# First conditioning round in two quarters and a half, and the filter network's middle layer moved

## The chip, the cores and the metric

The kernel runs on one core of one Trainium2 chip. The metric is device time of one execution in microseconds (us); lower is better. Engines in the text: PE multiplies matrices (PEld is its weight loading), DVE and ACT work element by element, POOL is a slower general engine, and SP issues the loads. Each engine takes its instructions in one fixed order, and an instruction whose input is late holds up everything behind it on that engine.

## The reference

One layer of a sequence model, over 512 latent tokens x and 256 context tokens of width 1024. The part that matters here is its beginning:

```python
mod = (silu_c @ w_ada[l] + b_ada[l])[:, None, :]
sh1, sc1, g1, sh2, sc2, g2 = jnp.split(mod, 6, axis=-1)
modc = silu_cc @ w_ada[l] + b_ada[l]
csh1, csc1, cg1, csh2, csc2, cg2 = jnp.split(modc, 6, axis=-1)
hc = rmsnorm(ctx_s, norm1_g[l]) * (1.0 + csc1) + csh1
khc, vhc, lgc = project_kvg(hc, lp, seq_conv)
st_f, st_b = context_states(khc, vhc, lgc)
h = rmsnorm(x, norm1_g[l]) * (1.0 + sc1) + sh1
kh, vh, lg = project_kvg(h, lp, lat_conv)
y = mixer(h, kh, vh, lg, st_f, st_b, lp, lat_conv, hyena_spectra(seq_len, lp))
```

`mod` is the conditioning: a vector from c times the wide matrix `w_ada`. Its first two sixths, the shift `sh1` and the scale `sc1`, are needed before h exists, and h feeds every projection. `hyena_spectra` runs a small filter network (three layers, each a product followed by a sine) over 512 positions and turns its output into spectra; it does not depend on x. Everything after the mixer (merge, output projection, gated feed-forward part, last norm) stays as it is.

## The kernel before, in words

**Layout.** x lies transposed in eight tiles `xt[k]` of 128 features by 512 tokens (buffers `uh`, `ul`). A product of fp32 precision is made of three products of split numbers: a number is split into a rounded high half and the rest, its low half, and `gemm` (L555) issues for each of the eight k high times high (L215), high weight times low input (L216) and low weight times high input (L217). So h needs a high half `hTh` (ACT, L1071) and a low half `hTl` (DVE, L1077, from an intermediate that DVE makes at L1076), and each weight tile needs a high half `wh` (ACT) and a low half `wl` (DVE).

**Conditioning.** Rows of `w_ada` for shift and scale are 4 MB. They come in two halves of 16 pieces of 256 KB: the first half serves the features of k = 0 to 3, the second those of k = 4 to 7. `ada_load` (L301) issues the loads of a half, into buffers that are free at that time (`hTh`, `hTl` and `K` for the first half; `hTh`, `hTl`, `dih`, `dil`, `gx1`, `cx2` for the second). `ada_first` (L315) multiplies them with the silu of c and of the context's c: 32 products 256 columns wide (64 matmul instructions in a trace), four side by side in PE's columns. ACT copies the result, PE transposes it twice (L328), DVE adds the bias into `modT` (L335) and makes the scale `amod` (L336).

**Start of x.** ACT squares the eight tiles, DVE adds the squares (L385), PE sums over the partitions with a matrix of ones (L388), DVE and POOL form the reciprocal root (L371, L373), PE spreads it over all partitions into the bank `xb` (L375), and DVE multiplies x by it (L1040 for k = 0 to 3, L1101 for k = 4 to 7).

**Query tiles.** The first four query weight tiles (0 to 3) are held in PSUM and made in two parts each: `part(i, 0)` takes k = 0 to 3, as soon as the first conditioning half is there, `part(i, 1)` takes k = 4 to 7. Each part is twelve matmuls. Between the first parts stand the first products of the filter spectrum (L445, L446) and the second half of conditioning; before its second use DVE normalises k = 4 to 7.

**Filter network.** `filter_network` (L392) is a generator: at each `next` it issues the sine of the layer before, the matmul of the next layer, and six dependent DVE operations (L407 to L412). The last layer is twice as wide as the first two. Its result, the stack, is what L445 and L446 multiply with the weights `w4`. The table of the transform (`fr`, split into `fh` and `fl`) is needed by the spectrum's later products only.

**What sets the order.** The program is written as one sequence. A planner then gives each engine its own fixed order: among the instructions of which it believes the inputs ready, the one that stands first in the program goes. `tc.issue_after(ins)` binds the instructions of its block that run on the engine of `ins` to come behind `ins` there, without a wait for its result. `behind(lag)` (L560) is the same for the last matmul of the list `tails`, to which `gemm` adds the last matmul of each call. Loads are issued by SP in program order.

## Time and profile before

| | |
|---|---|
| three runs | 1227.28, 1228.36, 1229.19 us (median 1228.36) |
| profiled execution | 1230.75 us |
| its span, first to last instruction | 1228.9 us |
| granted clock of PE, mean | 0.99 |
| PE busy | 1189.2 us, 97% |
| DVE busy | 834.1 us, 68% |
| ACT busy | 528.3 us, 43% |
| chain that ended last | PE 88%, DVE 5%, DMA 3% |

A row of the timeline reads: start in us from the beginning of the span, length in us, engine, line of the kernel, operation, tile written and tiles read, shapes, how many instructions of this kind follow each other, and, in brackets, how long the engine stood idle before and what ended that. Neighbouring instructions overlap by about a tenth of a microsecond. PEclk is the share of full speed that PE's clock was granted.

### The profile page before, as it was taken

To read this page: it belongs to the slowest core of one execution; us is meant where nothing else is said; L and a number is where in the kernel's file an instruction comes from. 1 tells how busy PE (TensorE), PEld (TensorE's weight loads), DVE (VectorE), ACT (ScalarE), POOL (GpSimd) and SP (SyncE) were. 2 spreads that over 40 slices of the span, in tenths; PEclk is the share of its full clock that TensorE was granted. 3 is DMA by queue.
4 is the path that set the end of the run, shared out by engine and by line. 5 is a ranking of instruction groups with operands and counts; after the bars stand their busy time and mean duration, and the time that the engine had idled before them with its cause. 6 is when DMAs were issued, how large, how long until landed. Compare 5 with 4: busy or idle time off the path is not lost.

```text
span 1228.9 us, 16765 instructions
## 1 busy us (share of the span) xinstructions
PE 1189.2 (97%) x6440; PEld 1014.0 (83%) x6440; DVE 834.1 (68%) x1336; ACT 528.3 (43%) x824; POOL 69.1 (6%) x131
## 2 busy tenths in 40 slices
PE   4999999999999999999999989999999999999997
PEld 2799988888888888888777878889888888888886
DVE  5967797978989899796767777667654344332332
ACT  3754466754445545354665633233423223222321
POOL 0011110100010000101001112000000000000000
PEclk9999999999999999999998999999999999999998
DMA  9644452463333443335645556773452332333312
GB/s 351 238 163 156 140 190 95 146 228 132 106 126 120 138 162 104 133 108 205 202 150 184 162 181 206 266 265 120 138 154 87 103 100 89 99 91 98 95 47 70
DMA packets 60689, 182.73 MB, mean 149 GB/s; under 512 B 8376, under 2 KB 12224, under 8 KB 58432
## 3 DMA queue, kind: packets, MB, share of 16 engines
q1 hardware_dynamic: 53264, 153.33, 38.5%
q0 software_dynamic: 7344, 28.32, 6.3%
q8 instruction: 51, 0.84, 0.3%
q14 instruction: 30, 0.25, 0.1%
HBM read 151.21 MB, written 30.41 MB: 148 GB/s over the span
## 4 chain that ended last, share of the span: by engine, by line
PE 88%; DVE 5%; DMA 3%; issue 2%; ACT 2%; POOL 0%; SPq 0%; DVEq 0%; POOLq 0%; ACTq 0%
PE bank L215 26%; PE bank L216 26%; PE bank L217 25%; PE bank L641 2%; PE bank L642 2%; PE bank L643 2%; DMA s<-hhd 1%; DMA wr<-in_wph 1%; PE bank L445 1%; PE bank L598 1%; PE bank L446 1%; DMA hmd<-s 1%; PE bank L319 1%; DVE wl L212 1%; DMA ul<-in_xT 0%
## 5 line engine op out<-in xcount | busy, mean ns | idle before, releaser
L215 PE MATMUL bank<-hTh,wh 128*128 128x512 f32 (+1 forms) x952 | 368.6, 389 | 7.5 <-DVE den L945 2.9
L216 PE MATMUL bank<-hTl,wh 128*128 128x512 f32 (+1 forms) x952 | 367.2, 387 | 2.0 <-DVE hTl L1077 2.0
L217 PE MATMUL bank<-hTh,wl 128*128 128x512 f32 (+1 forms) x952 | 367.0, 386 | 0.0
L211 ACT ACTIVATE wh<-wr 128x1024 fp32r<-128x1024 f32 (+1 forms) x167 | 172.1, 1032 | 407.9 <-PE bank L216 202.9
L212 DVE TENSOR_TENSOR wl<-wr,wh 128x1024 fp32r<-128x1024 f32 (+1 forms) x167 | 197.9, 1188 | 175.2 <-ACT wh L211 174.1
L215 PEld LDWEIGHTS bank<-hTh,wh 128*128 128x128 f32 x952 | 179.3, 189 | 43.6 <-issue 4.3
L216 PEld LDWEIGHTS bank<-hTl,wh 128*128 128x128 f32 x952 | 179.4, 189 | 36.7 <-DVE hTl L1077 2.5
L217 PEld LDWEIGHTS bank<-hTh,wl 128*128 128x128 f32 x952 | 179.4, 189 | 35.2
L216 PE MATMUL bank<-big,wh 128*128 128x512 f32 (+1 forms) x266 | 94.8, 356 | 0.0
L215 PE MATMUL bank<-big,wh 128*128 128x512 f32 (+1 forms) x266 | 94.7, 356 | 0.0
L217 PE MATMUL bank<-big,wl 128*128 128x512 f32 (+1 forms) x266 | 94.6, 356 | 0.0
L354 DVE SCALAR_TENSOR_TENSOR wr<-wr,crow 128x1024 f32<-128x1024 f32 x32 | 39.0, 1221 | 33.5 <-DMA wr<-in_wada 33.5
L216 PEld LDWEIGHTS bank<-big,wh 128*128 128x128 f32 x266 | 50.3, 189 | 7.1
L215 PEld LDWEIGHTS bank<-big,wh 128*128 128x128 f32 x266 | 50.3, 189 | 7.1
L217 PEld LDWEIGHTS bank<-big,wl 128*128 128x128 f32 x266 | 50.3, 189 | 7.1
L211 ACT ACTIVATE hb<-hb 128x512 fp32r<-128x512 f32 (+1 forms) x49 | 36.7, 768 | 28.0 <-DVE hb L450 17.7
L1525 DVE TENSOR_TENSOR s<-s,bank 128x512 f32<-128x512 f32 x22 | 15.1, 687 | 46.4 <-PE bank L217 46.4
L212 DVE TENSOR_TENSOR hb<-hb,hb 128x512 fp32r<-128x512 f32 (+1 forms) x49 | 40.3, 859 | 2.0 <-ACT hb L211 1.8
L643 PE MATMUL bank<-wh,hTl 128*128 128x256 f32 (+1 forms) x128 | 36.5, 285 | 0.0
L641 PE MATMUL bank<-wh,hTh 128*128 128x256 f32 (+1 forms) x128 | 36.5, 285 | 0.0
L642 PE MATMUL bank<-wl,hTh 128*128 128x256 f32 (+1 forms) x128 | 36.4, 284 | 0.0
L373 POOL TENSOR_TENSOR rr<-rv,negh 128x2 f32<-128x2 f32 (+1 forms) x6 | 5.5, 924 | 509.1 <-DVE rv L371 509.1
(376 smaller groups left out, 2194.0 us busy)
## 6 DMA issues: line engine op xcount, KB each, us to landing
wr<-in_win SPq DMA_DIRECT2D x64, 512.0 KB, 3.7
wr<-in_w SPq DMA_DIRECT2D x60, 512.0 KB, 3.6
wr<-in_wada SPq DMA_DIRECT2D x32, 512.0 KB, 4.4
Kd<-K POOLq DMA_DIRECT2D x8, 1024.0 KB, 4.7
K<-Kd SPq DMA_DIRECT2D x8, 1024.0 KB, 5.6
wr<-in_wv SPq DMA_DIRECT2D x8, 512.0 KB
gmd<-s POOLq DMA_DIRECT2D x16, 256.0 KB, 2.6
wr<-in_wph SPq DMA_DIRECT2D x8, 512.0 KB, 3.5
```

What stands on the lines that cost most here:

```text
L211: act.activation(hi, x, AF.Copy)
L212: dve.tensor_sub(lo, x, hi.bitcast(F32))
L215: pe.matmul(o, wh, xh, start=first, stop=False)
L216: pe.matmul(o, wh, xl, start=False, stop=False)
L217: return pe.matmul(o, wl, xh, start=False, stop=last)
L319: m = pe.matmul(ps[32 * g : 32 * g + 32, :256], silc[:, k, :], units[k, g], start=bool(k == 0), stop=bool(k == KT - 1))
L354: dve.scalar_tensor_tensor(w, w, 1.0, crow[:], op0=ALU.mult, op1=ALU.mult, accum_out=s)
L445: pe.matmul(ps[:], lhs, w4h, start=True, stop=False)
L641: pe.matmul(o, xh, wh, start=bool(k == 0), stop=False)
L642: pe.matmul(o, xh, wl, start=False, stop=False)
L643: m = pe.matmul(o, xl, wh, start=False, stop=bool(k == KT - 1))
L1525: dve.tensor_tensor(t[:], t[:], pb[:], op=ALU.mult)
```

## The change

The rows of `w_ada` for the first half are laid out as two quarters of eight pieces. Quarter 0 serves k = 0 and 1, quarter 1 serves k = 2 and 3; the second half (now parts 2 and 3 of the loads) stays whole. A quarter has 32 products of 128 columns, one transpose and one addition. Loads are issued in the order quarter 0, query tile 0, quarter 1, query tiles 1 to 3, spectrum vectors, second half, transform table, context.

In the program the middle layer of the network now stands ahead of quarter 0, and the last square, the sums and the broadcast are bound behind the transpose of quarter 0 on PE. x is normalised and h is made in pieces of two k. Tile 0's first part is cut in two (k = 0, 1 and k = 2, 3). The network's last layer is bound behind the first of these on PE. The second half's conditioning products stand behind tile 3's first part and the spectrum's first products in the program and are bound only behind tile 2's; the split of the transform table moves behind the high and low halves of k = 4 to 7.

```diff
-    w = a["w_ada"][0][:, :2048].reshape(4, 2, 128, 2, 2, 2, 256)
-    c["wada1"] = w.transpose(4, 0, 3, 2, 5, 1, 6).reshape(2, 4, 2, 128, 4, 256)
+    w = a["w_ada"][0][:, :2048].reshape(KT, 128, 2, 2, 2, 256)
+    q = w[:, :, :, 0].transpose(3, 0, 1, 2, 4).reshape(2, KT, 128, 512)
+    h = w[:, :, :, 1].reshape(KT, 128, 2, 512).transpose(2, 0, 1, 3)
+    c["wada1"] = np.concatenate([q, h], 0)
...
+    def ada_load(part):
+
+        for k in range(KT):
+            dma(aslots[part][k], I["wada1"][part, k])
+
+    def ada_first(part, p, tag):
+
+        n = 1 if part < 2 else 2
         ps = bank()
         for k in range(KT):
             for g in range(4):
...
+                u = aslots[part + (g // 2 if n == 2 else 0)][k]
+                c0 = 128 * n * (g % 2 if n == 2 else g)
+                pe.matmul(
+                    ps[32 * g : 32 * g + 32, : 128 * n], silc[:, k, :], u[:, c0 : c0 + 128 * n], start=bool(k == 0), stop=bool(k == KT - 1)
                 )
...
+        tails.append(mark.ins)
...
+    ada_load(0)
+    load_q(0)
+    ada_load(1)
+    for i in range(1, NQ):
+        load_q(i)
+    dma(w4r, I["hw4"][sp[0]].rearrange("p f n -> p (f n)"))
+    dec, skip = spectrum_vectors(PH, *sp[0])
+    ada_load(2)
+    ada_load(3)
+    dma(fr, I["dftf"])
...
+    for k in range(KT - 1):
         sq_sums(ax_, xt[k], k, 4, PH, "s2", sums)
     next(network)
-    ahead(AH[0])
+    am = ada_first(0, PH, "s2")
     xb = bank()
-    rms_bcast(sums[:, :4], 4, xb, PH, "s2")
-    next(network)
-    ahead(AH[1])
-    for k in range(4):
-        dve.tensor_tensor(xt[k], xt[k], xb[:], op=ALU.mult)
+    with behind():
+        sq_sums(ax_, xt[KT - 1], KT - 1, 4, PH, "s2", sums)
+        rms_bcast(sums[:, :4], 4, xb, PH, "s2")
...
-    high, low = modulated(0)
+    norm(0, 2)
+    list(early_split(0))
+    high, low = modulated(0, 2)
+    norm(2, 4)
+    ada_first(1, PH, "s2")
     qps = [bank(psG) for _ in range(NQ)]
     with tc.issue_after(high), tc.issue_after(low):
+        part(0, 0, 2)
+        high, low = modulated(2, 4)
+    with behind():
+        next(network)
+    with tc.issue_after(high), tc.issue_after(low):
         list(early_split(1))
+        list(early_split(2))
+        part(0, 2, 4)
+        part(1, 0, 4)
+        part(2, 0, 4)
         stack = next(network)
+        list(early_split(3))
...
+        norm(4, KT)
+        part(3, 0, 4)
     sp0 = spectrum(*sp.pop(0), (dec, skip, (w4s[:, 0], w4s[:, 1])))
-    for i in range(AQ):
-        part(i, 0)
-    next(sp0)
-    ada = ada_first(PH, 1, units[1], "s2")
-    tr, am, copy = ahead(8)
-    for i in range(AQ, NQ):
-        part(i, 0)
-    with tc.issue_after(high), tc.issue_after(low):
-        split(fh[:], fl[:], fr)
-    high, low = modulated(1)
+    with behind():
+        next(sp0)
+    with tc.issue_after(tails[-2]):
+        ada_first(2, PH, "s2")
+    high, low = modulated(4, KT)
...
     with tc.issue_after(high), tc.issue_after(low):
-        part(0, 1)
+        split(fh[:], fl[:], fr)
+        part(0, 4, KT)
...
```

116 lines of the change are left out of this document (38 added, 78 removed).

## The prediction

> **What bounds the kernel.** I read the page first: span, busy time, slices.
>
> ```profile
> span 1228.9 us, 16765 instructions
> PE 1189.2 (97%) x6440; PEld 1014.0 (83%) x6440; DVE 834.1 (68%) x1336; ACT 528.3 (43%) x824; POOL 69.1 (6%) x131
> ```
>
> PE is busy for 97% of the span. What it lacks lies at the start, so a change there is worth what it takes from, or adds to, the time PE loses before its matmul stream runs without holes. I then asked for the stages of the start in a table of windows: from the first matmul of the query tiles to the end of their second parts. Columns: stretch, its length, busy time and count of PE, PE's weight loads, DVE, ACT, POOL; granted clock; DMA share; GB/s.
>
> ```profile
> 29.73:32.45 2.72, 0.73 (x1) 0.23 (x2) 2.72 (x7) 2.72 (x4) 0.00 (x0) 0.52 1.02 385
> 32.45:36.60 4.15, 4.15 (x10) 3.28 (x11) 4.09 (x6) 4.11 (x8) 0.00 (x0) 0.50 1.05 387
> 44.49:48.08 3.59, 3.59 (x65) 1.98 (x64) 3.49 (x4) 0.00 (x0) 0.00 (x0) 1.00 1.09 368
> 48.08:51.18 3.10, 3.10 (x19) 2.54 (x16) 1.80 (x8) 1.66 (x3) 0.00 (x0) 1.00 0.63 148
> 51.18:63.37 12.19, 12.19 (x57) 9.75 (x56) 11.36 (x20) 10.93 (x21) 0.70 (x1) 1.00 0.16 36
> ```
>
> From 32.45 PE has no hole left in this table. Up to 36.60 it runs at a granted clock of 0.50: ten matmuls in 4.15, 0.415 each. Before 32.45 it waits. The timeline of all engines says for what:
>
> ```profile
> 8.70 3.71 SPq L310 DMA_DIRECT2D hTl<-in_wada  x4
> 15.27 1.87 PE L388 MATMUL bank<-mats,s 128*128 128x1 f32 x8 [7.84 <-DVE s L385]
> 15.49 0.33 SPq L307 DMA_DIRECT2D wr<-in_win  x1
> 16.15 2.36 SPq L310 DMA_DIRECT2D K<-in_wada  x4
> 17.49 1.01 POOL L373 TENSOR_TENSOR rr<-rv,negh 128x4 f32<-128x4 f32 x1 [16.65 <-DVE rv L371]
> 19.99 2.08 PE L375 MATMUL bank<-mats,rr 128*128 128x128 f32 x8
> 22.11 1.28 DVE L1040 TENSOR_TENSOR uh<-uh,bank 128x512 f32<-128x512 f32 x2 [1.42 <-PE bank L375]
> 24.75 2.10 PE L319 MATMUL bank<-K,silc 128*32 128x256 f32 x31
> 26.96 0.38 ACT L325 ACTIVATE s<-bank 128x256 f32<-128x256 f32 x1 [4.40 <-PE bank L319]
> 28.27 0.36 DVE L335 TENSOR_TENSOR modT<-bank,vecs 128x4 f32<-128x4 f32 x4
> 28.66 0.17 DVE L336 SCALAR_TENSOR_TENSOR amod<-modT,vecs 128x8 f32<-128x8 f32 x1
> 28.86 1.52 ACT L1071 ACTIVATE hTh<-uh,modT,amod 128x512 fp32r<-128x512 f32 x2 [1.52 <-DVE amod L336]
> 29.88 1.00 DVE L1076 TENSOR_SCALAR s<-uh,amod,modT 128x512 f32<-128x512 f32 x2
> 31.71 2.50 DVE L1077 TENSOR_TENSOR hTl<-s,hTh 128x512 fp32r<-128x512 f32 x4
> 32.45 0.80 PE L216 MATMUL bank<-hTl,wh 128*128 128x512 f32 x1 [1.99 <-DVE hTl L1077]
> ```
>
> Two branches meet. x is normalised from 22.11 on. The first conditioning half ends with its matmuls at 26.85, and copy, transposes, sum and `amod` take until 28.83; then come the high and low halves of h. Conditioning is late by 6.7 us, and it is late because 16 pieces of it and one weight tile must land first.
>
> **Step 1, the first quarter.** SP issues pieces in order. The first eight (`hTh`, `hTl`) are out when the group that starts at 8.70 ends; its last issue starts near 8.70 + 3.71 - 0.33 = 12.1. In the new order these eight are the whole first quarter. All sixteen and the tile are issued by 16.15 + 2.36 - 0.33 = 18.2, the same bytes as before, so the second quarter ends where the half ended. Issue to landing, from the views of the two tiles, `hTl` first, `K` second:
>
> ```profile
> DMA to landing us min/median/max: 5.4/5.5/7.1
> DMA to landing us min/median/max: 6.0/6.0/6.0
> ```
>
> So the first quarter lands at 17.6, the second at 24.2. The quarters' matmuls are twice as many and half as wide; I cost them at nothing, as they fit between landings (if that cover goes, at most the 3.59 of the 64 in the table; at least nothing).
>
> **Step 2, the sums.** The four matmuls with ones and the broadcast are now queued on PE behind the quarter's transpose. The quarter's last eight matmuls take 0.5 (31 took 2.10), copy and transpose at most 1.3 (26.96 to the sum at 28.27, two transposes then, one now), taken 1.0: the sums start at about 19.1 instead of 15.27. They take 1.87, rv and POOL 1.36 more (17.14 to 18.50), the broadcast 2.08: x is normalised from 24.5, 2.4 us later than before. The network's middle layer, moved ahead of them, leaves this chain, and its matmuls fill an idle PE: nothing.
>
> **Step 3, DVE becomes the bound.** From 24.5 DVE owes tile 0, and then tile 1, a list in program order. Rows for the two pieces not yet shown, the low half of a weight tile and the network's last layer (first and last of its six operations, with one 0.60 norm among them):
>
> ```profile
> 24.24 0.81 DVE L407 TENSOR_SCALAR hb<-bank,hb 128x512 f32<-128x512 f32 x1 [0.24 <-PE bank L404]
> 27.93 0.43 DVE L412 TENSOR_SCALAR hb<-hb 128x512 f32<-128x512 f32 x1
> 34.12 1.22 DVE L1050 TENSOR_TENSOR wl<-wr,wh 128x1024 fp32r<-128x1024 f32 x1
> ```
>
> Spacing: a low half of h 0.60 (four in 2.50, one alone 0.69), a norm the same 0.60, an affine step (L1076) 0.50, sum and `amod` 0.56 (28.27 to 28.83). Tile 0's first low half is ready at 24.5 + 2 x 0.60 + 0.50 + 0.69 = 26.9, against 31.71 + 0.69 = 32.4 before: PE starts 5.5 us earlier. But it gets six matmuls (k = 0, 1) and must wait again for the second quarter's. Four norms 2.4, four affine steps 2.0, four low halves 2.4, `amod` of the second quarter 0.5 and tile 1's weight low half 1.2 are 8.5: 33.0. The second quarter's own chain, 24.2 + 0.5 + 2.0 = 26.7, ends before DVE comes to it. The last layer is 28.36 - 24.24 - 0.60 = 3.5 more; before the change it sat in time in which DVE waited for conditioning, now it is behind tile 0's first part and ahead of the weights in program order. How the two mix, these rows show:
>
> ```profile
> 8.71 0.43 DVE L410 SCALAR_TENSOR_TENSOR hb<-hb 128x256 f32<-128x256 f32 x1
> 9.05 0.69 DVE L385 TENSOR_TENSOR s<-s,s 128x512 f32<-128x512 f32 x1
> 9.65 0.42 DVE L411 SCALAR_TENSOR_TENSOR hb<-hb 128x256 f32<-128x256 f32 x1
> ```
>
> Between two dependent operations of the network the planner puts another one that is ready. So tile 1's low half waits for one of the six, 0.43, more likely than for all: a dense stream from W = 33.4 (bounds 33.0 and 33.0 + 3.5 = 36.5).
>
> What is that worth? Spacing at full clock, first and last of tile 1's twelve matmuls:
>
> ```profile
> 37.02 0.40 PE L215 MATMUL bank<-hTh,wh 128*128 128x512 f32 x1
> 39.55 0.39 PE L217 MATMUL bank<-hTh,wl 128*128 128x512 f32 x1
> ```
>
> (39.55 - 37.02) / 11 = 0.23. At 33.4 the new kernel has issued 14 of 48 (tile 0, and the two of tile 1 that need no low half), the old one 3.3 (one at 29.73, then (33.4 - 32.45) / 0.415): 10.7 x 0.23 = 2.5 us ahead. The old one has still 3.2 us at clock 0.50 before it, each worth 1 - 0.23 / 0.415 = 0.45: 1.4. The new one pays for as much as it runs slow after W: nothing at best, its own 4.15 x 0.45 = 1.9 at worst; PE will have been half busy since 26.9, so I take half, 0.9. While PE waits for tile 1's low half, high parts of tiles 2 and 3 can go ahead: 0 to 1.2, taken 0.6. Lead: 2.5 + 1.4 - 0.9 + 0.6 = 3.6 (2.0 to 5.1).
>
> On the slow clock the Trainium skill, page "TensorE: Matmul & The Clock Gate", section "Part 1: The HAM clock gate", says that the full clock comes back after a busy free-running window of about 3.4 us, wherever the burst falls in it. By that rule a burst that finds PE cold pays 3.4 x 0.45 = 1.5 instead of my 0.9, an estimate, and the sum below would be -0.5; the trace's 4.15 at 0.50 is longer than one window and shorter than two, which agrees. Its section "Why this matters for your kernels" advises against idle gaps of some 3 us between bursts, and short bursts with gaps are what this change makes of the start; no row of the old trace shows bursts of this kind.
>
> **Step 4, the second half loses its cover.** Before, its 64 matmuls (44.49 to 48.08) are followed by tile 3's twelve, and these hide the chain to the next stage:
>
> ```profile
> 36.49 1.02 SPq L310 DMA_DIRECT2D cx<-in_wada  x2
> ...
> 48.22 0.39 ACT L325 ACTIVATE s<-bank 128x256 f32<-128x256 f32 x1 [5.68 <-PE bank L319]
> 48.89 0.38 PE L328 MATMUL bank<-mats,s 128*128 128x128 f32 x2
> 49.91 1.52 ACT L1071 ACTIVATE hTh<-uh,modT,amod 128x512 fp32r<-128x512 f32 x2 [1.30 <-DVE amod L336]
> 50.83 0.69 DVE L1077 TENSOR_TENSOR hTl<-s,hTh 128x512 fp32r<-128x512 f32 x1
> 51.18 1.07 PE L215 MATMUL bank<-hTh,wh 128*128 128x512 f32 x4
> ```
>
> Now tile 3 and the spectrum's eight matmuls stand ahead of conditioning in program order, and nothing behind it can run before h. From 48.08 to the first high half of k = 4, 49.91 + 0.80 = 50.71 (two take 1.52), less the 0.28 that the transposes waited for PE (48.61 to 48.89): 2.35 us of idle PE. The four high matmuls (L215 x4) then cover the low half at 51.5. Bounds: nothing, if conditioning is placed ahead of tile 3; 51.52 - 48.08 - 0.28 = 3.2, if those four are not put in front. Taken 2.35. Its data: the last pieces were issued by 36.49 + 1.02 - 0.33 = 37.2 and landed 5.5 later, 42.7; the spectrum's table (128 x 1,280 x 4 bytes, 1.7 us at the table's 387 GB/s) no longer stands ahead of them: 41.0. PE begins the 64 at 33.4 + 34 x 0.23 + 0.9 - 0.6 + 8 x 0.23 = 43.4, so they don't wait.
>
> **Step 5, the spectrum's table.** Its split moves behind the second half's h:
>
> ```profile
> 43.91 1.48 DVE L212 TENSOR_TENSOR dfl<-hb,dfh 128x1280 fp32r<-128x1280 f32 x1
> ```
>
> DVE then gets 1.48 more in a stretch where it is busy 11.36 of 12.19, and the context's sums, which wait for DVE, come up to 1.5 later. PE has tile matmuls to run meanwhile unless they are queued behind: 0 to 1.5, taken 0.15. SP's queue: loads of later weights are behind the same bytes, nothing.
>
> **Sum.** -3.6 + 2.35 + 0.15 = -1.1 us. The profiled execution took 1230.75 (1.85 outside its span of 1228.9), so 1229.65 there; the runs' median, 2.39 lower, is 1228.36, so 1227.3 for the new runs.
>
> **Rivals.**
> A. The second half's matmuls are placed between tiles 2 and 3. For it: they are only held behind tile 2, and would come first if tile 3's low half were late in the planner's order. PE comes to tile 3 at 33.4 + 22 x 0.23 + 0.9 = 39.4; DVE still owes the rest of the layer 3.1, two weight halves 2.4 and the stack 0.7, 39.6 at the latest: close, and against it that the weight halves slip in between the layer's operations. The hole of step 4 is then covered by tile 3's twelve (2.8): -3.6 + 0.15 = -3.45, 1224.9. Near the same figure comes without it if PE keeps its full clock and more of tiles 2 and 3 goes ahead.
> B, slower. The network's last layer goes whole ahead of tile 1's low half on DVE. Then W = 36.5; the old kernel has issued 10.8 by then, the new one 14: 0.7, minus 1.9 for a cold restart after the long hole, so the lead is -1.2, and with steps 4 and 5 the kernel is 3.7 us slower: 1232.1. It decides from about W = 35.4 (old 8.1, so 1.4 + 0.5 - 1.9 = 0.0 of lead). For it: program order; against: the interleaved rows above.
> C. The quarter does not do what it says: matmuls of the second quarter are put ahead of the broadcast on PE, which then waits for data until 24.2 to 24.6. Normalising starts at 24.6 + 2.08 = 26.7, W = 35.6, and the lead, (14 - 8.6) x 0.23 + 0.45 - 0.9 + 0.6 = 1.4, is eaten by the hole: +1.1, 1229.5. For it: POOL's 1.36 us leave a gap that the planner fills; against: only as many as fit, and the first pieces land in time.
>
> **How the numbers follow.** This kernel can be told from no change beyond 0.2%, 2.46 us. Forecast (-1.1, own range -2.9 to +0.6) 0.42; A 0.30; B 0.14; C 0.14. Faster: 0.27 of A and 0.07 of the forecast, 0.34. Slower: 0.11 of B, 0.03 of C and 0.01 of the rest, 0.15. The rest, 0.51, is no change. The range runs from 1223.4 (A with the lead at its upper bound, 5.1) to 1231.3, where B's slow restart is about two thirds of what I take; it leaves out half of B and little else.
>
> **What would show it.** Right: first low-half matmul of tile 0 near 27, six matmuls, holes until about 33, tile 0 done before 32.5; normalising starts at 24 to 25; the 64 matmuls of the second half begin near 43 behind the spectrum's first products, with PE idle for about 2.3 us after them; tiles' second parts start 1 to 2 us before 51.18. Wrong: no hole after the 64 (A); DVE with six network operations in a row ahead of a weight split and PE idle past 35 (B); a broadcast that waits for a DMA (C).

## The result, and the profile after

The changed kernel takes 1235.26 us (median of 6 runs, 1232.09 to 1238.43), the kernel before 1227.82 beside it on the same chip (6 runs, 1226.81 to 1229.19). The ratio is 1.0057 (95% interval 1.0045 to 1.0070): slower by about 7 us, by more than the 0.2% that can be told from no change. I had forecast 1227.3. Times, here and below, are of executions in the usual state of the chip; two of the kernel before beside one set of experiments, at 1980 and 2396 us, are left out.

The profiled execution took 1238.43. Its page, span and busy line:

```profile
span 1236.7 us, 16888 instructions
PE 1194.2 (97%) x6504; PEld 1017.1 (82%) x6504; DVE 833.7 (67%) x1333; ACT 530.9 (43%) x827; POOL 71.1 (6%) x131
```

PE has 5.0 us more of busy time than before: 64 short matmuls more (6504 for 6440) and, for the rest, presumably matmuls that last longer at a lower clock (0.988 in the mean, 0.990 before). The span grew by 7.8, so PE also idles longer. The table of windows of the start, columns as in the prediction (busy time of PE, PEld, DVE, ACT, POOL; clock; DMA share; GB/s), says where:

```profile
40.00:45.00 5.00, 3.23 (x15) 2.39 (x14) 3.31 (x7) 2.64 (x4) 0.00 (x0) 1.00 1.03 391
45.00:50.00 5.00, 4.84 (x70) 2.65 (x68) 4.97 (x7) 0.00 (x0) 0.00 (x0) 1.00 1.00 299
50.00:55.00 5.00, 1.12 (x4) 0.79 (x5) 2.05 (x8) 2.46 (x5) 0.00 (x0) 0.93 0.02 7
55.00:60.00 5.00, 5.00 (x18) 4.00 (x17) 4.81 (x9) 3.77 (x7) 0.00 (x0) 0.73 0.00 0
```

PE was busy throughout these 20 us before. Now there is a hole in the first slice, a larger one in the third, where PE works 1.12 of 5 us, and a granted clock of 0.93 and 0.73 behind it. The timeline of after shows the first hole; the rows are in order of time, on DVE, ACT and PE:

```profile
39.69 0.69 DVE L400 SCALAR_TENSOR_TENSOR hb<-hb 128x512 f32<-128x512 f32 x1
40.29 0.68 DVE L1070 TENSOR_TENSOR uh<-uh,bank 128x512 f32<-128x512 f32 x1
40.89 0.42 DVE L401 TENSOR_SCALAR hb<-hb 128x512 f32<-128x512 f32 x1
41.35 0.63 ACT L403 ACTIVATE hb<-hb 128x512 f32<-128x512 f32 x1 [0.59 <-DVE hb L401]
41.99 0.39 PE L219 MATMUL bank<-hTh,wl 128*128 128x512 f32 x1
43.31 0.69 DVE L409 TENSOR_TENSOR astack<-hb,s 64x512 fp32r<-64x512 f32 x1 [0.81 <-ACT s L408]
44.15 0.47 PE L434 MATMUL bank<-hb,astack 128*128 128x512 f32 x1 [1.77 <-DVE astack L409]
```

The last first-part matmul of a query tile starts at 41.99. The next work on PE is the spectrum's, and its input `astack` is the result of the network's last layer, which comes 1.77 us too late. The layer's sine (L403) waits for DVE, which puts two weight splits, the split of the spectrum's weights and two of the norms of k = 4 to 7 (L1070) between the layer's six operations: these stretch from 34.23 to 41.31, 7.1 us, where they took 4.1 before (24.24 to 28.36). The second hole of after, behind the 64 conditioning matmuls of the second half (46.18 to 49.85):

```profile
43.83 2.18 SPq L419 DMA_DIRECT2D fd<-in_hdec  x1
49.46 0.39 PE L310 MATMUL bank<-cx,silc 128*32 128x256 f32 x2
51.54 0.63 ACT L414 ACTIVATE fd<-fd 128x512 f32<-128x512 f32 x1 [8.26 <-DMA fd<-in_hdec]
52.08 0.37 ACT L314 ACTIVATE s<-bank 128x256 f32<-128x256 f32 x1
52.49 0.44 PE L317 MATMUL bank<-mats,s 128*128 128x128 f32 x2 [2.65 <-ACT s L314]
53.45 1.52 ACT L1053 ACTIVATE hTh<-uh,modT,amod 128x512 fp32r<-128x512 f32 x2 [1.00 <-DVE amod L326]
54.31 2.07 PE L217 MATMUL bank<-hTh,wh 128*128 128x512 f32 x4 [1.38 <-ACT hTh L1053]
```

The products are done at 49.46 + 0.39 = 49.85, but the copy that carries them on (L314) starts at 52.08. In front of it in ACT's fixed order stands an Abs on `fd`, the decay vector of the *next* spectrum, and this waits 8.26 us for a load. The load is not later than before: it is issued at 43.83 now, at 43.76 before. But before the change the Abs stood elsewhere, as the view of the tile `fd` in the old trace shows (count, duration, first and last start):

```profile
L425 ACT ACTIVATE fd<-fd x1: 627/627/627, 61.9 to 61.9; 128x512 f32<-128x512 f32 x1
```

It ran at 61.9, behind the second half's conditioning and long after its data came. So the second parts of the tiles begin at 54.31 instead of 51.18.

To follow the lag through the kernel I take one row that all kernels have, a split of weights on DVE about 105 us in, behind the same wait in each. In the kernel before:

```profile
104.59 1.23 DVE L212 TENSOR_TENSOR wl<-wr,wh 128x1024 fp32r<-128x1024 f32 x1 [4.66 <-ACT wh L211]
```

And in the kernel after:

```profile
109.22 1.22 DVE L214 TENSOR_TENSOR wl<-wr,wh 128x1024 fp32r<-128x1024 f32 x1 [4.66 <-ACT wh L213]
```

Of the 7.8 us in span, 4.63 are there at 105 us. The other 3.2 arise between 620 and 740 us, where the program was not changed.

### The profile page after: what moved, and what is told of

It is laid out like the page before. It is cut to its first block, busy times and chain, and to the rows that moved or that the text cites. A ratio compares the mean times of both kernels' runs of the same rounds, so it can differ in the third digit from the quotient of the medians.

```text
span 1236.7 us, 16888 instructions
## 1 busy us (share of the span) xinstructions
PE 1194.2 (97%) x6504; PEld 1017.1 (82%) x6504; DVE 833.7 (67%) x1333; ACT 530.9 (43%) x827; POOL 71.1 (6%) x131
## 4 chain that ended last, share of the span: by engine, by line
PE 54%; issue 33%; DVE 3%; DMA 3%; POOL 2%; ACT 1%; SPq 0%; POOLq 0%; DVEq 0%
PE bank L217 16%; PE bank L218 15%; PE bank L219 15%; PE bank L631 2%; PE bank L630 2%; PE bank L632 2%; DMA gmd<-s 1%; POOL gmd L680 1%; DMA fd<-in_hdec 1%; DMA hmd<-s 0%; POOL kd L650 0%; DVE wl L214 0%; DMA wr<-in_wph 0%; PE bank L434 0%; POOL od L680 0%
```

## Experiments

All kernels were timed against the kernel before in five rounds. "Lag" is the start of the row above minus 104.59; "second high half" is the start of the first high part of h for k = 4 to 7 on ACT (49.91 before, 53.45 after). My theory after the trace: the loss at the start is the second half's conditioning without cover, made worse by two steps that stand ahead of it, the Abs on ACT and the network's late last layer. Rivals: the half clock behind the hole, the later split of the transform table, and a start that is no worse with all the loss in the tail.

### The Abs behind the copy

```diff
-        act.activation(dec[:], dec[:], AF.Abs)
+        with tc.issue_after(copies[-1]):
+            act.activation(dec[:], dec[:], AF.Abs)
```

> The kernel after, with one binding: the next spectrum's absolute value on ACT may not stand ahead of the copy of the second half's conditioning rows. Theory: the start gained what was forecast, and it is lost behind the first half, part of it where this copy (52.08 in the profile of after) stands behind an absolute value that waits for its DMA until 51.54. Then the copy comes at about 49.9, the second parts start at 49.9 + 2.23 = 52.1 instead of 54.31, and if the shorter hole also keeps the clock (it showed 0.73 in 55 to 60 us), another 1.4 us is saved: value heads from 68.5 to 69.9 instead of 72.05, time 1231.7 to 1233.2. Rival 1, the loss lies in the sums, the power on POOL (1.86 us) and the broadcast at 20 to 26 us: nothing changes, 1235. Rival 2, something else holds the second parts (the loads of the half): the copy moves but the second parts stay at 54.

Measured: 1234.88 us, ratio 1.0051 (1.0039 to 1.0063). The rows of ACT in its timeline:

```profile
51.38 0.38 ACT L314 ACTIVATE s<-bank 128x256 f32<-128x256 f32 x1 [6.63 <-PE bank L310]
52.77 1.52 ACT L1054 ACTIVATE hTh<-uh,modT,amod 128x512 fp32r<-128x512 f32 x2 [0.35 <-DVE amod L326]
```

The copy now waits for PE, not for the load, and follows the last product at once. But in this execution the start was 1.5 us later (the second quarter's transposes at 30.47 instead of 28.91, because its matmuls ran at half clock), so the second high half came only 0.7 earlier. The lag is 3.97. From the end of the 64 matmuls to the second parts it takes 2.3 us here (51.32 to 53.63) instead of 4.5 (49.85 to 54.31). So the Abs is a cause, and alone it is worth less than the scatter of the start lets one see in the total; the forecast of 1231.7 to 1233.2 was missed.

### The second half's products ahead of tile 3 again

```diff
         norm(4, KT)
+        with behind():
+            ada_first(2, PH, "s2")
         part(3, 0, 4)
...
-    with tc.issue_after(tails[-2]):
-        ada_first(2, PH, "s2")
```

> The kernel after, with the second half's conditioning matmuls, its copy and its additions traced ahead of the fourth projection tile's first half (bound behind the third tile) instead of behind it and the filter's first matmuls. Theory: both holes (1.77 us at 42.2 for the filter stack, 4.0 us of idle time at 49.85 to 54.31) go, since the fourth tile and the eight filter matmuls cover the stack's chain and the conditioning's chain: third tile ends at 39.5, 64 matmuls to 43.2 if their loads are in, fourth tile to 45.9, filter to 47.8, second parts from 47.8 instead of 54.31; value heads from 65 to 67 instead of 72.05; time 1227.5 to 1230.5. Rival 1 (the loss is made ahead of 30 us): unchanged, 1235. Rival 2, the loads of the second half land too late for this place: PE waits for them at 39.5 and second parts come at 50 or later, 1231 to 1233.

Measured: 1229.32 us (12 runs), ratio 1.0013 (1.0003 to 1.0023). Undoing this one placement takes back nearly the whole loss. Tile 3's matmuls cover the chain again, the second high half starts at 45.42, both holes are gone and the clock stays at 1.00. But that is 4.5 us earlier than before the change, and the kernel is not faster. The lead of PE itself is smaller, since the 64 matmuls now stand ahead of tile 3: its second parts begin at 48.47 instead of 51.18, 2.7 us earlier. Three of its windows:

```profile
50.00:55.00 5.00, 5.00 (x24) 4.14 (x23) 4.91 (x8) 2.85 (x7) 0.00 (x0) 1.00 0.03 7
55.00:60.00 5.00, 4.55 (x21) 3.42 (x19) 4.97 (x7) 4.73 (x10) 0.00 (x0) 1.00 0.01 2
60.00:65.00 5.00, 4.21 (x29) 3.84 (x30) 4.97 (x8) 3.41 (x5) 0.00 (x0) 1.00 0.48 137
```

The first matmul of its second parts, and its matmuls that waited between 58 and 70 us:

```profile
48.47 0.40 PE L217 MATMUL bank<-hTh,wh 128*128 128x512 f32 x1
60.41 0.98 PE L630 MATMUL bank<-wh,hTh 128*128 128x272 f32 x4 [0.87 <-ACT wh L213]
61.77 0.39 PE L631 MATMUL bank<-wl,hTh 128*128 128x272 f32 x1 [0.38 <-DVE wl L214]
67.52 0.71 PE L364 MATMUL bank<-mats,rr 128*128 128x128 f32 x4 [0.39 <-POOL rr L362]
```

DVE is busy 4.91 to 4.97 of every 5 us. PE comes to the value weights and to the context's normalisation before DVE and ACT have split the one and summed the other. The waits of 0.87, 0.38 and 0.39 take 1.6 of the 2.7 us of lead; where the rest goes is not shown. The lag at 105 us is -0.47. That DVE is what takes the lead is argued from its windows; no run made DVE's work less.

### The network's last layer in the wait for the broadcast

```diff
+        if between:
+            with tc.issue_after(m.ins):
+                tails.append(between())
...
-    norm(0, 2)
+    with behind():
+        norm(0, 2)
...
-    with behind():
-        next(network)
```

`between` is the layer; it is bound behind the reciprocal root's DVE step and ahead of the normalisation.

> The kernel after, with the filter network's last layer put into the wait for the broadcast (its matmul ahead of the broadcast's, its six DVE steps between the sums' rv and the normalisation) instead of behind the first tile. Theory: the normalisation comes at 26.6 instead of 26.2, DVE has 3.4 us less to do from 33 to 41, the sine needs no second table load (1.28 us), the filter stack is there before the fourth tile ends, and the copy of the conditioning rows comes ahead of the next absolute value: no hole at 42.2, conditioning matmuls end at 47.8, second parts from about 50.1 instead of 54.31, value heads from 66.5 to 68, time 1229.5 to 1231. Rival (what binds the start is DVE ahead of the first low half): the delay of 0.5 us or more runs through and outweighs the table load; the first tile starts 1 us or more later, and the time stays within 1 us of 1235.

Measured: 1235.46 us, ratio 1.0052 (1.0034 to 1.0069), no gain. The stack's hole is gone and the copy starts 2.9 us earlier. The first parts end later, though, with their last matmul at 43.28 instead of 41.99, and the Abs has moved on to the next place where it hurts:

```profile
49.20 0.38 ACT L314 ACTIVATE s<-bank 128x256 f32<-128x256 f32 x1 [6.75 <-PE bank L310]
52.69 0.63 ACT L417 ACTIVATE fd<-fd 128x512 f32<-128x512 f32 x1 [3.11 <-DMA fd<-in_hdec]
53.23 1.50 ACT L1056 ACTIVATE hTh<-uh,modT,amod 128x512 fp32r<-128x512 f32 x2
54.08 1.70 PE L217 MATMUL bank<-hTh,wh 128*128 128x512 f32 x4 [4.00 <-ACT hTh L1056]
```

PE idles 4.00 us in one piece for a load that nothing near it needs. One of the two causes alone uncovers the other; the load sets the time.

### Both of these moved: the layer early, and the products ahead of tile 3

The last two edits together.

> Both of the last two edits: the network's last layer in the wait for the broadcast, and the second half's conditioning ahead of the fourth tile. Theory: the holes are gone with the second edit alone, so this is within 1 us of that kernel (second parts from about 47.8, value heads from 65 to 67, time 1227 to 1230.5). Rival: DVE's 3.4 us from 33 to 41 still held the second half's normalisation in that kernel; then this one is faster than it by 1 to 3 us.

Measured: 1234.43 us, ratio 1.0051 (1.0036 to 1.0066). The second high half starts at 47.05, with no hole before it. PE then waits 1.82 us for the first value weight's high half and 1.31 us for the context's root (at 63.22 and 66.38; POOL takes 1.68 us for this root, and 0.70 in the changed kernel), the clock between 65 and 70 us is 0.66, and the lag is 4.39. The same loss as in the changed kernel, 10 us further on, with a start that looks better. This I had not expected.

### The layer early, and the Abs behind the second half's high parts

```diff
-        act.activation(dec[:], dec[:], AF.Abs)
+        with tc.issue_after(marks[-1]):
+            act.activation(dec[:], dec[:], AF.Abs)
```

on top of the layer's edit above; `marks` holds the last high part of the second half.

> The kernel with the network's last layer in the wait for the broadcast, and the next spectrum's absolute value bound behind the second half's last high part on ACT. In the kernel without this binding the conditioning rows' copy came at 49.2, and ACT then stood 3.11 us at the absolute value, whose DMA landed at 52.7, so the second parts started at 54.08. Theory: the wait for that DMA is the second half's bound; without it the second parts start at 51.5 (49.64 for the transposes and 1.8 behind them), the hole is 2.4 us instead of 5, value heads 2.6 to 4 us earlier, time 1231.5 to 1233. Rival: another wait takes its place (DVE's low halves, or the value heads' weights), and the time stays at 1235.

Measured: 1234.17 us, ratio 1.0038 (1.0025 to 1.0050). Both of the steps ahead of the chain are gone:

```profile
49.84 0.38 ACT L314 ACTIVATE s<-bank 128x256 f32<-128x256 f32 x1 [7.62 <-PE bank L310]
51.23 1.52 ACT L1057 ACTIVATE hTh<-uh,modT,amod 128x512 fp32r<-128x512 f32 x2 [1.00 <-DMA fd<-in_hdec]
52.10 1.88 PE L217 MATMUL bank<-hTh,wh 128*128 128x512 f32 x4 [1.38 <-ACT hTh L1057]
```

(The releaser of the second row is one of several that ended close together; L1057 reads `uh`, `modT` and `amod`, not `fd`.) The second parts begin at 52.10, 2.2 us earlier than in the changed kernel, and the lag is 2.44, also 2.2 less. That is the two queued steps, 1.9 + 2.2 = 4.1, less what the layer's new place and a half-clock window cost in front of them: tile 0's first low half is used at 31.75 instead of 30.51, the clock is 0.5 until 35.25, and the last matmul of the first parts starts at 43.93 instead of 41.99, 1.9 us later. The hole that is left is the one I had forecast (0.5 + 1.4 of waits and the transposes), and with the half clock behind it, it still eats more than the lead.

### Unread matmuls in the hole

The changed kernel, with 11 matmuls ahead of the second half's transposes and 5 behind them, whose bank nothing reads:

```diff
+    def keep(ins, n):
+        d = bank()
+        with tc.issue_after(ins):
+            for _ in range(n):
+                pe.matmul(d[:], early[0][0][:, 0], hT[0][0][:], start=True, stop=True)
```

> The kernel after, with 16 matmuls that nobody reads (128x512, 0.23 us each) put into the hole at 49.85 to 54.31: 11 behind the second half's conditioning matmuls, 5 behind its transposes. They fill a wait and move no other work. Theory: the clock falls to 0.73 in 55 to 60 us because TensorE stood for 4 us, and that costs 1.3 to 2 us on top of the hole; with the array kept busy the second parts still start at about 54.3, but run at 0.23 us a matmul at once, and the value heads start 1.3 to 2 us earlier than 72.05: 70 to 70.7, time 1233 to 1234. Rival (the clock's fall there is not made by the hole): value heads stay at 72, time 1235.

Measured: 1234.41 us (1233.96 to 1242.10), ratio 1.0061 (1.0041 to 1.0082). The clock is 1.00 from 45 to 70 us, and yet the lag is 5.29:

```profile
54.98 1.20 PE L217 MATMUL bank<-hTh,wh 128*128 128x512 f32 x4 [0.22 <-ACT hTh L1064]
65.76 1.68 POOL L373 TENSOR_TENSOR rr<-rv,negh 128x2 f32<-128x2 f32 x1 [41.46 <-DVE rv L371]
67.50 0.71 PE L375 MATMUL bank<-mats,rr 128*128 128x128 f32 x4 [0.80 <-POOL rr L373]
```

PE runs at full clock into the context's root, which hangs on the same late h through the orders of ACT and DVE, and waits 0.80 us for it. But POOL took 1.68 us for the root in this execution, and 0.70 in the changed kernel, so most of this wait is not the price of a late h. With a root of 0.70 the lag would be about 4.5, and it began 0.66 later than in the changed kernel (54.11 for 53.45): by this estimate the fall of the clock is worth up to 0.8 us of the lag. Why the root took longer is not shown. The rival "it is the clock" falls as the whole cause, and stands as a part of it.

### The table's split ahead of the second half's h

The kernel with the layer early and the Abs behind, and the split of the transform table put back ahead of the second half's modulation:

```diff
+    with tc.issue_after(high), tc.issue_after(low):
+        split(fh[:], fl[:], fr)
     with tc.issue_after(tails[-2]):
         ada_first(2, PH, "s2")
```

> The kernel with the network's last layer in the wait and the absolute value bound behind the second half (lag of 2.4 us over before at 105 us), and the DFT table's split put back in front of the second half's modulation. Theory: from the start of the second half's modulation to the context's broadcast the time is a chain on ACT and DVE of fixed length (13.7 us from the copy to the context's sums in two kernels), and the change lengthened it by the table's split, 1.26 us on ACT and 1.48 us on DVE, which before lay at 41.3 to 45.4 ahead of the modulation. Then the lag at 105 us falls from 2.4 to between 0.9 and 1.2, time about 1.3 us less than that kernel's 1234.2: 1232.5 to 1233.3, give or take one slow clock window (1.7 us) of the late heads. Rival (the table's split costs 0.15 us, as forecast): lag 2.2 to 2.4, time 1234.

Measured: 1234.68 us, ratio 1.0045 (1.0033 to 1.0057). The second high half came at 51.86 and no window at half clock followed, but PE waited at the context's root:

```profile
65.15 0.71 PE L367 MATMUL bank<-mats,rr 128*128 128x128 f32 x4 [1.03 <-POOL rr L362]
```

The lag is 3.03, and the forecast of 0.9 to 1.2 was missed. The root comes 65.15 - 51.86 = 13.3 us behind the second high half, as in the kernel with the filled hole (67.50 - 54.11 = 13.4), and as there POOL took longer for it (1.78 us). So no gain from the table's place is seen, but this pair does not price it: the two profiles differ by a half-clock window and by 1 us of POOL as well.

### The value weights earlier as well

The products ahead of tile 3, and load and split of the first value weights traced ahead of the context's sums:

```diff
+        vw0 = v_weights(0)
         csums, cb_ = bank(), bank()
...
-        v_head(PH, h, v_weights(h))
+        v_head(PH, h, v_weights(h) if h else vw0)
```

> The kernel with the second half's conditioning ahead of the fourth tile, and the value weights' load and split traced ahead of the context's sums. In the kernel without this second edit TensorE led before by 3.9 us at 58 us, and lost 1.7 to 2 us of it between 59 and 68 us, waiting for the value weights' halves (ACT at 59.25, DVE at 60.43, behind the spectrum's halves and the context's sums) while DVE had worked without a pause from 45.4. Theory: the order on DVE is what takes the lead back; with the weights' halves first the waits at 60.4 and 61.8 go (1.25 us), time 1227.5 to 1228.5. Rival: DVE is full whatever the order, and the wait moves to the spectrum's or the context's halves; time within 0.6 of 1229.3.

Measured: 1228.24 us (11 runs), ratio 1.0000 (0.9991 to 1.0008). The two waits at 60 us are gone, only 0.42 us for the context's root is left, the lag is -1.27. This is the best version with the quarters, and it equals the kernel before.

### All of it together

Layer early, products ahead of tile 3, value weights early, table early.

> Four edits together: the network's last layer in the wait for the broadcast, the second half's conditioning ahead of the fourth tile, the DFT table's split ahead of the second half's modulation, the value weights' split ahead of the context's sums. In the kernel with the first two DVE stood idle for 4.7 us at 41.9 to 46.6 and was full from there to 67 us, and lost all it had gained between 60 and 70 us. Theory: what is moved into that idle time (the table's 1.48 us) and the earlier weights take the waits of 60 to 70 us away: lag at 105 us of -2.5 to -1, time 1226 to 1228, the same as before or 0.1 to 0.2% faster. Rival: DVE's order behind the second half still sets the value heads, lag 0 or above, time 1229 or more.

Measured: 1230.65 us (12 runs, 1225.96 to 1233.86), ratio 1.0008 (0.9992 to 1.0024); lag -0.11. Not faster than the kernel before, where 1226 to 1228 was forecast. No version beat it.

### A plain delay in the kernel before

Twenty unread matmuls behind the first half's last tile of the kernel before, 4.5 us of PE (from 50.07 to 54.60 in its trace):

```diff
+    d = bank()
+    for _ in range(20):
+        pe.matmul(d[:], early[0][0][:, 0], hT[0][0][:], start=True, stop=True)
```

> The kernel before with nothing of the change, and 20 matmuls that nobody reads (0.2275 us each, 4.55 us) behind the first half's last tile, so that all later work stands 4.55 us later without a hole. In the profile of after the lag of 4.6 us at 100 us grew to 7.6 at the end, all of it between 620 and 740 us. Theory: that growth is the clock of the later heads, where holes fall otherwise against the clock's own windows when all work is shifted; then this kernel's runs scatter more than 4.55 over before, from 0 to 3 us: 1232 to 1236, with a lag that changes between 620 and 740 us. Rival (the growth has a cause in the change itself): the lag stays at 4.55 from 60 us to the end, time 1232.7 within 0.5.

Measured: 1232.54 us, ratio 1.0030 (1.0019 to 1.0042), 3.8 us over the kernel before in its batch; lag 3.44. A late start passes to the end about one for one and does not grow by itself. So the changed kernel's lag of 4 to 5 us at 105 us explains 4 to 5 of its 7, not all.

### Both kernels once more

The two kernels unchanged, for a second profile of each.

> The kernel after once more, unchanged. In ten profiles the granted clock falls to a half only in windows of 3.41 us on one grid, and between 620 and 740 us the profiles have from 2 to 5 such windows (before 3, after 5). Theory: each is worth 1.7 us, their number differs from run to run of the same kernel, and the lag made ahead of 105 us is the change's own cost: 4.2 to 5.3 us again at 105 and at 600 us, and span = 1228.9 + lag + 1.7 x (windows - 3), windows from 2 to 5, not necessarily 5. Rival (the five windows belong to the change): 5 windows again and a span of 1236 to 1237.

> The kernel before once more, unchanged, for the same question: windows at half clock between 620 and 740 us may be 1 to 5 instead of 3; span = 1228.9 + 1.7 x (windows - 3) within 0.5 us. If before shows 3 or fewer each time and after 5 each time, the tail is a cost of the change whose way is not understood.

Measured: after 1235.37 (ratio 1.0052, 1.0035 to 1.0070), before 1228.38 (0.9992, 0.9981 to 1.0004). The lag is 4.12 and -1.15. In the second profile of after, the Abs stands ahead of the copy again (51.16 and 51.70) and the second parts begin at 53.93. The rule put down ahead of these two, a span of 1228.9 plus the lag plus 1.7 for each window more than three, gives 1234.7 for after with its four windows, and for before, put down without a lag, 1228.9 with its three; the spans are 1233.7 and 1227.1, both outside the 0.5 us that I had allowed for before.

### Filling two holes in the tail

In every trace PE has holes near 627 us, 650 and 722, and windows at half clock can follow. In the kernel before, first the end of the hole near 627 and then the edges of the window behind it:

```profile
629.54 0.50 PE L215 MATMUL bank<-hTh,wh 128*128 128x512 f32 x1 [2.27 <-ACT hTh L211]
630.63 0.63 PE L217 MATMUL bank<-hTh,wl 128*128 128x512 f32 x1
...
634.02 0.40 PE L215 MATMUL bank<-uh,K 128*128 128x512 f32 x1
```

After 2.27 us of idle PE the matmuls last 0.63 instead of 0.40, for 3.4 us. Such windows I count in the windows table: a clock of 0.91 in 20 us is one. The kernel before in three stretches of the tail:

```profile
660.00:680.00 20.00, 20.00 (x107) 16.31 (x106) 12.58 (x25) 10.78 (x22) 1.66 (x3) 1.00 0.49 170
700.00:720.00 20.00, 19.41 (x109) 16.71 (x110) 12.51 (x23) 10.06 (x18) 1.67 (x3) 1.00 0.78 249
720.00:740.00 20.00, 16.06 (x110) 14.71 (x109) 16.83 (x46) 8.45 (x18) 4.28 (x8) 1.00 0.29 94
```

And the kernel after in the same:

```profile
660.00:680.00 20.00, 20.00 (x111) 16.79 (x110) 13.50 (x35) 9.48 (x22) 5.37 (x6) 0.95 0.69 220
700.00:720.00 20.00, 19.18 (x91) 15.35 (x91) 12.69 (x30) 10.87 (x25) 2.82 (x6) 0.91 0.67 213
720.00:740.00 20.00, 17.49 (x106) 15.78 (x106) 15.23 (x31) 8.86 (x16) 0.80 (x4) 0.91 0.43 143
```

Ahead of these, from 620 to 640 and from 640 to 660 us, the clock is 0.91 and 0.83 before, 0.86 and 0.93 after. So from 620 to 740 us the kernel before has three windows of half clock in its first profile, the changed one five. In three kernels (after, before, and the products ahead of tile 3 with the value weights early) I put 10 unread matmuls into the first hole and 17 into the second:

```diff
+                keep(m.ins, 10, wh[:, 0], hh[0][0][:])
...
+        if (h, d) == (1, 0):
+            keep(tails[-1], 17, piece(wh, d, 4)[:, 0 - PIECE[d][4][0]], Vh[:, 4])
```

> The kernel after, with matmuls that nobody reads put into two late holes: 10 (0.23 us each) into the wait for the seventh high half of the first gated tile (2.7 us at about 632), and 17 (0.12 us each) into the wait for the second head's low values (2.1 us at about 656). In every profile the half-clock windows between 620 and 660 us follow these two holes. Theory: the holes make them; with the array busy the windows at 630 to 662 go, and this kernel gains 3 to 5 us on after, 1230 to 1232. If the 2 us that after loses beyond its lag at 105 us (1235.3 against 1228.4 by the medians, lag 4.4 by the profiles) are made by these windows, it then stands 4.4 to 5.2 over before with the same edit. Rival (the clock falls anyway, or the work behind the holes waits for other engines): 1235 as after.

> The kernel before with the same two fillings and nothing of the change. Theory: its three half-clock windows at 630 and 651 to 658 go, worth 1.7 us each at most: 1223.5 to 1226 against 1228.4. Rival: other engines set the time there, 1228.

> The same two fillings in the kernel with the second half's conditioning ahead of the fourth tile and the value weights' split ahead of the context's sums (1228.2, lag of -1.3 us at 105 us in its profile). Theory: as with before, 2 to 5 us less: 1223 to 1226, at or below before with the fillings. Rival: 1228.

Measured: 1234.78 (ratio 1.0047, 1.0031 to 1.0063), 1228.44 (0.9997, 0.9988 to 1.0006) and 1229.63 (1.0009, 1.0000 to 1.0018); all three forecasts of a gain were missed. The clock is 1.00 from 620 to 720 us in after and before with the fillings, and near 666 us the lag of these two is 2.9 and 2.7 us less than at 600; but by 733 us 2.1 and 1.6 of that are given back, at the hole near 722 us (3.20 us in after and 2.79 in before with the fillings) with a half-clock window behind it. None is faster than its unfilled twin beyond the scatter, and 6.3 us remain between the filled pair.

### The runs side by side

Growth is the difference of the spans (to 1228.9) minus the lag at 105 us, which is what the rest of the kernel adds; windows are those at half clock from 620 to 740 us in that profile.

| kernel | median us | second high half | lag | growth | windows |
|---|---|---|---|---|---|
| before, two profiles | 1227.8, 1228.4 | 49.91, 48.76 | 0, -1.15 | 0, -0.7 | 3, 3 |
| after, two profiles | 1235.3, 1235.4 | 53.45, 53.06 | 4.63, 4.12 | 3.2, 0.7 | 5, 4 |
| Abs behind | 1234.9 | 52.77 | 3.97 | -0.3 | 3 |
| layer early | 1235.5 | 53.23 | 4.43 | 3.0 | 5 |
| layer early, Abs behind | 1234.2 | 51.23 | 2.44 | 2.9 | 5 |
| same, table early | 1234.7 | 51.86 | 3.03 | 2.1 | 5 |
| hole filled | 1234.4 | 54.11 | 5.29 | -1.7 | 2 |
| ahead of tile 3 | 1229.3 | 45.42 | -0.47 | 0.2 | 3 |
| same, value weights early | 1228.2 | 46.45 | -1.27 | 1.3 | 3 |
| both moved | 1234.4 | 47.05 | 4.39 | -0.6 | 3 |
| all together | 1230.7 | 47.11 | -0.11 | -0.8 | 2 |
| before, delayed | 1232.5 | | 3.44 | -2.8 | 2 |

In the kernels with the hole, the lag goes with the second high half: 53.45 to 4.63, 51.23 to 2.44, 54.11 to 5.29, each 48.8 apart. In two of them, the hole filled and the table early, no half-clock window follows, but there PE waits 0.80 and 1.03 us for a root that took POOL 1 us longer. And the growth goes with the number of windows, about 1.5 us each.

## Why the prediction was wrong, point by point

**Steps 1 and 2** held in order and were late in size. Rows of after:

```profile
19.93 1.87 PE L377 MATMUL bank<-mats,s 128*128 128x1 f32 x8 [1.06 <-DVE s L374]
22.15 1.86 POOL L362 TENSOR_TENSOR rr<-rv,negh 128x4 f32<-128x4 f32 x1 [21.31 <-DVE rv L360]
24.06 2.08 PE L364 MATMUL bank<-mats,rr 128*128 128x128 f32 x8 [2.27 <-POOL rr L362]
27.40 1.05 PE L310 MATMUL bank<-K,silc 128*32 128x128 f32 x32
30.51 0.50 PE L218 MATMUL bank<-hTl,wh 128*128 128x512 f32 x1 [0.39 <-DVE hTl L1059]
```

The sums start at 19.93 (forecast 19.1), since DVE's last addition of squares stood behind the quarter's `amod`. POOL took 1.86 for an operation of the same form that took 1.01 before. The broadcast therefore starts at 24.06, x is normalised from 26.18 (forecast 24.5), and the second quarter's 64 matmuls, which I cost at nothing, wait behind the broadcast on PE and end at 28.45. On ACT the copy of these products stands in front of the first high half of h, which so starts at 28.75, although its x is normalised by about 26.9:

```profile
28.58 0.28 ACT L314 ACTIVATE s<-bank 128x128 f32<-128x128 f32 x1 [8.78 <-PE bank L310]
28.75 1.51 ACT L1053 ACTIVATE hTh<-uh,modT,amod 128x512 fp32r<-128x512 f32 x2
```

The first low half is used at 30.51, not 26.9: 1.9 us instead of 5.5 earlier than before. This is the fault of step 4 in small: I followed the chain of one quarter and not what the other quarter's copy holds up.

**Step 3**, the lead, came out as forecast in size and otherwise in kind; that the size agrees is luck. The half clock, of which I took 0.9, did not occur; from 30.84 the matmuls last 0.40, and all 48 of the first parts are issued by 41.99 + 0.23 = 42.2. Before, the second parts started at 51.18 behind the same 48, the spectrum's eight (8 x 0.23) and the 64 (3.59): 45.7 without these. The lead is 3.5, forecast 3.6 (2.0 to 5.1). Less was done early and it was done at full clock. The tiles did not find PE cold: the broadcast and the second quarter's products had kept it busy from 24.06, and the first sixteen of these took 0.86 us (26.07 to 26.93), the next sixteen 0.47. The Trainium skill's rule in "Part 1: The HAM clock gate" of "TensorE: Matmul & The Clock Gate", by which I charged 1.5 to a burst that finds PE cold, agrees with this trace in so far as the full clock came back within a busy stretch; in the first experiment half clock did hold up the second quarter. Where the window's edge falls differs from run to run, so no single figure was right.

**Step 4** is the step that failed: "The second half loses its cover ... Taken 2.35." Its own sum is the path from the 64 matmuls to h, and that path was right: with the steps ahead of it removed, waits of 0.50 and 1.38 were left, and it took 2.3 us (49.78 to 52.10). What I did not do is go through the other queues in which the moved step now stands. Two things were ahead of it:
- The layer whose result the spectrum's first products need was moved as well, behind tile 0's first matmuls. With the spectrum now ahead of the 64 on PE, a late stack holds these up too: 42.2 to 44.15, 1.9 us. I had seen the layer only as a load on DVE in front of a weight split. (ACT also has to load its table for the sine again, 1.28 us from 39.47; that ends at 40.75, before DVE is done at 41.31, and costs nothing here.)
- An Abs of the next spectrum came ahead of the copy on ACT, presumably because the planner thought its input ready sooner, and it waits for a load of 7.7 us from issue: 49.85 to 52.08, 2.2 us.

So the hole is 49.85 to 54.31, 4.5 us, and the start of the second parts is -3.5 + 1.9 + 0.2 (spectrum and products a little longer) + 4.5 = +3.1 against 51.18, which is the 54.31 seen. A half-clock window behind it costs 1.7 more (3.4 us at half speed), 4.8 in all against the 4.63 of the row at 105 us. My upper bound for this term, 3.2, was the worst case of the one chain that I followed; it was no bound for the queues.

The experiments bear this out by taking the parts away: both queued steps removed, the lag falls by 2.2, with 1.9 lost again ahead of them; the cover given back, it falls by 5.1, to -0.47. The window alone is not the cause: with it filled, the lag did not fall, in part because the context's root took 1 us longer. What the window is worth by itself is not shown exactly: PE loses 1.7 us in it, and by the estimate above up to 0.8 of that is still there at 105 us.

**Step 5**, 0.15, is not contradicted: putting the table's split back brought no gain, but its price was not measured apart from the rest.

**The sum's frame** was wrong too, and no row of the first 55 us would have shown it. I counted a lead of PE at 51 us as a gain at the end. In the kernel with the cover given back PE led by 2.7 us at the start of the second parts, and 0.47 of that were left at 105 us, no more than the second profile of before has (1.15); DVE was busy for 4.91 to 4.97 of every 5 us in between. Even a right step 4 would have given a small gain or none; the best variant of this change is at 1.0000. Nor does what PE lacks lie at the start alone, as I had it: of its 39.7 us without work in the profile before, 18.5 lie ahead of 32.45, 9.9 between 620 and 740 us and 8.4 behind 1210.

**The rivals.** A (the 64 between tiles 2 and 3) did not happen by itself; when I wrote it into the program it gave 1229.3, not 1224.9, as its lead of 2.7 us was lost again. B and C did not happen: the network's operations were interleaved with weight splits as forecast, and the broadcast waited for POOL, not for a DMA.

**What stays open.** At 105 us the three profiles of after (4.63, 4.12 and, with the tail's holes filled, 4.31) and of before (0, -1.15, -0.83) lie 5.0 us apart; the medians differ by about 7. The other 2 arise from 620 to 740 us, where all kernels have the same order of instructions. In the profiles they go with the number of half-clock windows, five and four in the two plain profiles of after, three in both of before. But the first profile of after is of the slowest of its six executions, and over all executions the clock does not tell the kernels apart: its mean is 0.9913 and 0.9918 in the two sets of after, 0.9904 to 0.9911 in the sets of before beside the experiments. Even if the half clock at the start is taken out (one window in after, two in before, by the profiles), the time lost to the clock in the rest differs by some 0.7 us, an estimate from these means. So the windows explain at most a part of the 2 us, and the rest stays open: the kernel before with a plain delay of the same size had two windows, and with two of the holes filled the distance is still 6.3.

## What to carry to other kernels

When a step is moved behind others, list for every engine on its chain what now stands in front of it in that engine's fixed order, and what each of these waits for; an instruction that waits for a load it doesn't need soon is harmless in one place and costs its whole wait in another. A hole's price is the chain plus these, so an upper bound from the chain alone is none. And before a lead is counted as a gain, find the next stretch in which another engine is full: there the lead ends.

## What the runs showed of the hardware

Half clock came in windows of 3.4 us (630.6 to 634.0 above), one or two of them behind a hole, and all windows of one profile lay on one grid of that length, whose place differs from run to run. That agrees with the free-running window in the Trainium skill, "TensorE: Matmul & The Clock Gate", section "Part 1: The HAM clock gate". The Trainium skill's advice to avoid gaps of some 3 us (same page, section "Why this matters for your kernels") is not strict enough for this kernel: 2.27 us of idle was enough near 627 us, while 1.77 us near 43 us was not. One window costs 1.7 us if PE is the bound, and two or three more or fewer of them make most of the scatter of several us between executions of one kernel: among the twelve of "all of it together" the mean clock is 0.994 to 0.995 in the four fastest (1225.96 to 1226.97 us) and 0.989 in the two slowest (1233.82 and 1233.86), and 0.0055 of 1230 us is 6.8 of the 7.4 us between them. Keeping the clock up with unread matmuls worked in each hole that was filled, and never made the kernel faster.

POOL's reciprocal root does not take a fixed time for its shape. At the start of x, on 128x4, it took 1.01 us in all four profiles of the kernel before and its variants, and 1.86 in all thirteen of the changed kernel and its variants. For the context, on 128x2, it took 0.70 to 0.73 us in most, and 1.68 to 1.78 in three (the hole filled, both moved, the table early). So this goes with the program more than with chance, and by what is not shown; where PE waits for it, it is up to 1 us of the start.
